# Preparing the scan operators of a two-layer hybrid backbone on VectorE alone, beside the Fourier mixer, with other amounts of gate work beside the scan of layer two

## The chip, the core and the metric

One core of a Trainium2 chip runs the kernel. The metric is the time of one execution in microseconds on the device, the median of several. Lower is better. The engines are TensorE (PE; its weight loads are listed as PEld), VectorE (DVE), ScalarE (ACT), GpSimd (POOL) and SyncE (SP), which here issues the DMA transfers.

## What is computed

Two layers work on 256 context tokens and 512 latent tokens of width 1024. Each layer normalises its tokens, projects them once, and feeds four mixers: A, latent attention; B, a Fourier transform over tokens and channels; C, a diagonal state space in both directions (S5); D, retention. Each mixer's 256 columns go through a branch matrix, are multiplied by a sigmoid gate, and are summed:

```python
o = jnp.stack([o_a, o_b, o_c, o_d], axis=2)
y = jnp.einsum('blnw,nwd->blnd', o, w_branch)
g = jax.nn.sigmoid(gates.reshape(B, L, N_BRANCH, D_MODEL))
return jnp.sum(g * y, axis=2) @ w_out
```

A residual and a squared-ReLU feed-forward part of width 4096 follow. Mixer C is the one that the change touches:

```python
lam = lax.complex(lam_re, lam_im);  step = jnp.exp(log_step)[:, None]
lam_bar = jnp.exp(lam * step)
b_bar = ((lam_bar - 1.0) / lam)[..., None] * lax.complex(b_re, b_im)
bu = jnp.einsum('blgh,gph->blgp', u, b_bar)        # 16 groups of 16 channels, 64 states
_, xs = lax.associative_scan(linear_recurrence_op, (lam_bar, bu), axis=1)
y = einsum(xs_f, c_f).real + einsum(xs_b, c_b).real + d * u
val, gate = jnp.split(gelu(y) @ w_glu, 2, axis=-1);  out = val * sigmoid(gate)
```

## The kernel before

**Matrix products.** A float32 product is made of three products of rounded parts. A weight tile `raw` comes by DMA from SyncE, ScalarE rounds it to `whi`, VectorE subtracts to `wlo` (`split`, line 300). Gates use tiles of 128x1024 (`raw`, `whi`, `wlo`); branch matrices use 128x256 (`raws`, `whis`, `wlos`), and there is one buffer of `raws`, so the next transfer waits until both parts of the last are made. In layer 0 a gate is 48 matmuls; in layer 1, where only the latent tokens are kept, 24. A branch tile (`br`) is 12 and 6.

**Merging a mixer.** `merge_steps` is a generator that makes, for one mixer, a gate (matmuls, then a tanh on ScalarE) or a branch tile (matmuls, then VectorE's `gate<-gate,mm` or `xy<-gate,mm`, and, except for the first mixer, GpSimd's `xy<-xy,gate`) at each step. The argument `lead` says how many gates are made before the first branch tile. TensorE fills gaps of other stages with such steps.

**The scan.** The state space is done in chunks of eight tokens with 96 chunks. For each of eight groups (two of the reference's groups each) it needs small operators: `R` (128x288), `Wr` and `Wi` (128x256, made from Vr, Vi, wr, wi), a strip `ks`, all written to DRAM, and the rotation factors `er`, `ei` (16 x 96 per partition) of all groups, made by doubling: 1, 2, 4, 8, 16, 32 and again 32 columns, each in six products and sums with `gr`, `gi`, which are then squared. `s5_scalars` makes the small parameters (`par`), `s5_rot` the rotations, `s5_ops` the operators. In `s5_ops`, `first(g)` is the VectorE and GpSimd part, `second(g)` the TensorE and ScalarE part: eight products into one PSUM tile, then four transposes into another, both from `pb`, a pool of two buffers named `b`.

**Which engine.** Lines 1503 to 1535 give 10 of 16 columns of each longer rotation step to VectorE and 6 to GpSimd; `first` gives `Wi` to GpSimd (`e2`), and `second` the two sums of `ks`.

**Where it stands in the order.** `self.bg` is a background generator and `tick(n)` takes n of its steps; a scheduler orders each engine's instructions from there. Layer 0: `s5_prep`, which takes one step of the rotation and one of the operators by turns, runs under `merge_b`, the merge of mixer B behind the Fourier mixer (about 97 to 200 us). Behind it come `ada`, the other modulation rows (line 497), on VectorE too. Layer 1: `prepare(1)` runs in the feed-forward part of layer 0; there `f2`, the second product, also takes its accumulators `b` from `pb`, and VectorE adds them as `xy<-b,mod,xy`. In the scan itself (`s5`), `S5_STEPS[l][i]` steps of merges A and C are taken beside each group i; `early` is how many gates of merge C may be made there, before the scan's output exists. What is left of merge C follows the scan.

Of the kernel before, what the change touches and what calls it, by code (L numbers as in the profile page):

```python
# [33 lines left out]
FH = 258  # L34
# [6 lines left out]
S5_STEPS = ((2, 2, 1, 2, 1, 2, 1, 2, 1, 1, 1, 1), (2, 2, 2, 2, 2, 2, 2, 2, 2, 1, 1, 1))  # L41
# [174 lines left out]
class Net:  # L216
# [283 lines left out]
    def start(self, sp, prm):  # L500
# [38 lines left out]
        def scalars():  # L539
            for _ in range(4):  # L540
                next(later)
# [117 lines left out]
    def layer(self, l):  # L659
# [8 lines left out]
        with tc.tile_pool(name=f"mix{l}", bufs=1) as mp:  # L668
# [28 lines left out]
            early = 7 if last else 3  # L697
# [127 lines left out]
    def prepare(self, l):  # L825
# [16 lines left out]
    def merge_steps(self, l, n, o, segs, lead=1):  # L842
# [7 lines left out]
        for m in range(KT + lead - 1):  # L850
            if m < KT:
# [3 lines left out]
                g = Cols(self.mp.tile([128, NTOK - self.c0], F32, name="gate", bufs=7 if last else 3), self.c0)  # L855
# [27 lines left out]
    def fnet(self, l, sp, segs, o, gates):  # L883
# [31 lines left out]
        next(gates)  # L915
        T = {}
# [18 lines left out]
        for t in range(2):  # L935
            self.ahead['fl', t] = self.chunk(('fl', t), [sp.tile([128, 2 * FH], F32R, name=f"f{x}{t}") for x in ("hi", "lo")])
        next(gates)
        for s0, s1 in segs:
# [18 lines left out]
            for j in range(2):  # L957
# [10 lines left out]
                self.split(o[j][0][:, s0:s1], o[j][1][:, s0:s1], v)  # L968
        next(gates)
# [370 lines left out]
    def s5_scalars(self, l, sp):  # L1340
# [34 lines left out]
        self.tt(qi, qi, t0, OP.mult)  # L1375
        qb = lambda t: t[:, :, None].to_broadcast([128, 16, 16])
# [30 lines left out]
    def s5_prep(self, l, sp):  # L1407

        nc = self.nc
        bc = sp.tile([128, 2, 16, 16], F32, name="bc")  # L1410
        nc.sync.dma_start(bc, self.s5p[l][:, 512:])
        par = sp.tile([128, 16 * NPAR + 48], F32, name="par")
        nc.sync.dma_start(par, self.par[l])
        pr, pi, wr, wi, Br, Bi, Vr, Vi, rot = self.par_views(par)
# [5 lines left out]
        todo = [self.s5_rot(l, sp, rot), self.s5_ops(l, sp, bc, pr, pi, wr, wi, Br, Bi, Vr, Vi, dd)]  # L1420
        while todo:
            for t in list(todo):
                if next(t, 0) is None:
                    yield
                else:
                    todo.remove(t)

    def s5_ops(self, l, sp, bc, pr, pi, wr, wi, Br, Bi, Vr, Vi, dd):
        nc = self.nc
# [3 lines left out]
        def first(g):  # L1433
            gs = slice(2 * g, 2 * g + 2)
            e1, e2 = nc.vector, nc.gpsimd
# [5 lines left out]
            self.tt(Rr, c4(0), s4(pr), OP.mult, e1)  # L1441
            self.tt(t[0], c4(1), s4(pi), OP.mult, e1)
            self.tt(Rr, Rr, t[0], OP.subtract, e1)
            self.tt(Ri, c4(0), s4(pi), OP.mult, e1)
            self.tt(t[1], c4(1), s4(pr), OP.mult, e1)
            self.stt(Ri, Ri, -1.0, t[1], OP.mult, OP.subtract)

# [12 lines left out]
        def second(g, R, Wr, Wi):  # L1460
# [269 lines left out]
```

## Time and profile before

| | us |
|---|---|
| median of 3 runs | 2232.37 |
| lowest and highest | 2227.95, 2234.98 |
| the profiled execution | 2233.41 |
| its span | 2231.6 |
| TensorE busy | 2150.9 |
| VectorE busy | 1443.6 |
| ScalarE busy | 760.8 |
| GpSimd busy | 242.2 (283 instructions) |

The span is that of the profile; the execution's own time is longer by 1.8 us. TensorE is at 2.4 GHz when its granted clock is written as 1.00 and at 1.2 GHz when it is 0.50; values between are means over a stretch. The mean over the span is 0.988.

### The profile page before, as it was taken

The page shows a single profiled execution, that of the slowest core. Times are in us where ns is not written, and L with a number is a line of the kernel's source. Part 1 is how long each engine was busy: PE and PEld are TensorE (multiplying, and loading weights), DVE is VectorE, ACT ScalarE, POOL GpSimd, SP SyncE. Part 2 cuts the span into 40 slices and gives each one's busy share as a digit, 9 for nine tenths or more (in the row PEclk, how much of TensorE's full clock was granted, in tenths as well). Part 3 has the DMA queues.
Part 4 walks back from the last instruction along what each step waited for, and adds up shares of the span by engine and source line. Part 5 has one row for each costly group of instructions (what it writes and reads, how often), then busy time and mean ns, then how long its engine had stood idle before and what let it go on. Part 6 is the DMA issues. An engine that isn't in the chain of part 4 may idle for free.

```text
span 2231.6 us, 32342 instructions
## 1 busy us (share of the span) xinstructions
PE 2150.9 (96%) x12366; PEld 1828.5 (82%) x12366; DVE 1443.6 (65%) x3215; ACT 760.8 (34%) x1306; POOL 242.2 (11%) x283
## 2 busy tenths in 40 slices
PE   7988999999999999999999999999999989999999
PEld 1877987888888888888878788987788869888887
DVE  6587889976735576676885447568746656544454
ACT  2322433444433332121222235434534434222322
POOL 2062001100212000000131101100011111000000
PEclk8999999999999999999999999999999999999999
DMA  8345233313323145545232332112134332333332
GB/s 268 110 121 147 81 109 118 124 48 116 95 80 119 66 142 161 168 128 177 97 110 77 93 119 81 43 54 78 53 120 120 112 114 74 98 101 96 95 95 94
DMA packets 117769, 239.93 MB, mean 108 GB/s; under 512 B 16208, under 2 KB 45552, under 8 KB 117616
## 3 DMA queue, kind: packets, MB, share of 16 engines
q1 hardware_dynamic: 117616, 237.89, 34.3%
q8 instruction: 97, 1.59, 0.3%
q14 instruction: 56, 0.46, 0.1%
HBM read 218.29 MB, written 19.55 MB: 107 GB/s over the span
## 4 chain that ended last, share of the span: by engine, by line
PE 76%; DVE 13%; issue 5%; DMA 3%; ACT 3%; POOL 1%; SPq 0%; ACTq 0%; POOLq 0%; DVEq 0%
PE mm L245 48%; PE b L245 25%; PE b L248 3%; DVE wlo L300 1%; DVE olo L497 1%; DVE xy L261 1%; DVE R L251 1%; ACT whi L299 1%; DMA raw<-wst 1%; DMA adp<-wst 0%; POOL hlo L251 0%; ACT tmp L264 0%; DVE gate L261 0%; DMA par<-par 0%; DVE er L251 0%
## 5 line engine op out<-in xcount | busy, mean ns | idle before, releaser
L245 PE MATMUL mm<-hhi,wlo 128*128 128x256 f32 (+1 forms) x1768 | 533.2, 356 | 6.1 <-DVE wlo L300 4.5
L245 PE MATMUL mm<-hlo,whi 128*128 128x256 f32 (+1 forms) x1768 | 532.9, 355 | 3.3 <-POOL hlo L251 3.2
L245 PE MATMUL mm<-hhi,whi 128*128 128x256 f32 (+1 forms) x1768 | 532.4, 355 | 0.0
L300 DVE TENSOR_TENSOR wlo<-raw,whi 128x1024 fp32r<-128x1024 f32 (+2 forms) x233 | 292.2, 1255 | 161.8 <-ACT whi L299 161.2
L245 PEld LDWEIGHTS mm<-hhi,wlo 128*128 128x128 f32 x1768 | 331.1, 189 | 54.2 <-issue 4.0
L245 PEld LDWEIGHTS mm<-hlo,whi 128*128 128x128 f32 x1768 | 332.6, 189 | 51.5 <-POOL hlo L251 6.2
L245 PEld LDWEIGHTS mm<-hhi,whi 128*128 128x128 f32 x1768 | 332.5, 189 | 46.2
L299 ACT ACTIVATE whi<-raw 128x1024 fp32r<-128x1024 f32 (+2 forms) x233 | 243.2, 1046 | 370.8 <-PE b L245 307.7
L245 PE MATMUL b<-uh,wlo 128*128 128x256 f32 (+1 forms) x704 | 215.3, 360 | 9.6 <-DVE xy L261 6.6
L261 DVE SCALAR_TENSOR_TENSOR xy<-b,mod,xy 128x256 f32<-128x256 f32 (+1 forms) x192 | 121.9, 659 | 149.0 <-PE b L245 148.9
L245 PE MATMUL b<-ul,whi 128*128 128x256 f32 (+1 forms) x704 | 215.6, 359 | 0.1
L245 PE MATMUL b<-uh,whi 128*128 128x256 f32 (+1 forms) x704 | 215.0, 359 | 0.0
L245 PEld LDWEIGHTS b<-uh,wlo 128*128 128x128 f32 x704 | 132.4, 190 | 34.0 <-DVE xy L261 6.9
L251 DVE TENSOR_TENSOR tmp<-tmp 128x768 f32<-128x768 f32 (+1 forms) x64 | 52.8, 824 | 163.9 <-ACT tmp L264 163.9
L245 PEld LDWEIGHTS b<-ul,whi 128*128 128x128 f32 x704 | 132.8, 189 | 21.1 <-DVE ul L300 0.8
L264 ACT ACTIVATE tmp<-mm 128x768 f32<-128x768 f32 (+3 forms) x86 | 51.5, 599 | 289.0 <-PE mm L245 269.8
L245 PEld LDWEIGHTS b<-uh,whi 128*128 128x128 f32 x704 | 133.0, 189 | 20.0
L251 POOL TENSOR_TENSOR xy<-xy,gate 128x768 f32<-128x768 f32 (+1 forms) x48 | 84.6, 1765 | 544.3 <-DVE gate L261 449.8
L245 PE MATMUL mm<-whi,hlo 128*128 128x256 f32 (+1 forms) x424 | 122.9, 290 | 0.6 <-ACT tmp L264 0.6
L245 PE MATMUL mm<-wlo,hhi 128*128 128x256 f32 (+1 forms) x424 | 122.1, 288 | 0.6 <-DVE wlo L300 0.5
L245 PE MATMUL mm<-whi,hhi 128*128 128x256 f32 (+1 forms) x424 | 121.8, 287 | 0.0
L264 ACT ACTIVATE gate<-mm 128x768 f32<-128x768 f32 (+1 forms) x64 | 45.0, 702 | 150.9 <-PE mm L245 142.7
(459 smaller groups left out, 3365.5 us busy)
## 6 DMA issues: line engine op xcount, KB each, us to landing
raw<-wst SPq DMA_DIRECT2D x236, 512.0 KB
adr<-wst SPq DMA_DIRECT2D x96, 256.0 KB
olo<-wst SPq DMA_DIRECT2D x42, 256.0 KB
adp<-wst SPq DMA_DIRECT2D x32, 256.0 KB
raws<-wst SPq DMA_DIRECT2D x64, 128.0 KB
xy<-xT SPq DMA_DIRECT2D x16, 384.0 KB
ohi<-wst SPq DMA_DIRECT2D x22, 256.0 KB
oB<-scr SPq DMA_DIRECT2D x16, 294.0 KB
```

The lines of the kernel that those rows point to most:

```text
L245: return self.nc.tensor.matmul(out, a, b, start=start, stop=stop)
L248: self.nc.tensor.transpose(out, a, self.ident[:n, :n])
L251: (eng or self.nc.vector).tensor_tensor(out=out, in0=a, in1=b, op=op)
L261: (eng or self.nc.vector).scalar_tensor_tensor(out, a, s, b, op0=op0, op1=op1)
L264: self.nc.scalar.activation(out, a, f, **kw)
L299: self.last_hi = self.nc.scalar.activation(hi, src, AF.Copy)
L300: return (eng or self.nc.vector).tensor_tensor(out=lo, in0=src, in1=hi.bitcast(F32), op=OP.subtract)
L497: self.nc.vector.tensor_tensor_reduce(out=junk, in0=r, in1=c[:, v], scale=1.0, scalar=0.0, op0=OP.mult, op1=OP.add, accum_out=acc[:, v:v + 1])
```

## The change

Nothing that is computed changes. In layer 0 the rotations run under the Fourier mixer (`fnet` has new `tick` calls) and the operators alone under `merge_b`; in layer 1 all rotations come before all operators. GpSimd has no part in either: rotation steps are 16 columns wide on VectorE, and `Wi` and the sums of `ks` are on VectorE. `first` is two steps, `s5_scalars` eight instead of four. `second` puts its transposes into the upper half of each bank of the PSUM tile that its products use. To make room, the Fourier mixer's second table reuses the buffers of its folded input (`u`). In layer 1, four gates of merge C instead of seven are made beside the scan, with four buffers, and three of its groups take one step instead of two.

```diff
-S5_STEPS = ((2, 2, 1, 2, 1, 2, 1, 2, 1, 1, 1, 1), (2, 2, 2, 2, 2, 2, 2, 2, 2, 1, 1, 1))
+S5_STEPS = ((2, 2, 1, 2, 1, 2, 1, 2, 1, 1, 1, 1), (2, 2, 2, 2, 1, 2, 1, 2, 1, 1, 1, 1))
...
-            with tc.tile_pool(name=f"fn{l}", bufs=1) as sp:
-                self.fnet(l, sp, segs, o_b, merge_b)
-            self.dump2(f'ob{l}', o_b)
-            self.bg = iter(())
+            with tc.tile_pool(name=f"rot{l}", bufs=1) as rp:
+                self.bg = iter(()) if l else self.s5_prep(l, rp)
+                with tc.tile_pool(name=f"fn{l}", bufs=1) as sp:
+                    self.fnet(l, sp, segs, o_b, merge_b)
+                self.dump2(f'ob{l}', o_b)
+                self.tick(99)
+                self.bg = iter(())
+                if l == 0:
+                    with tc.tile_pool(name="sp0", bufs=1) as sp:
+                        self.bg = self.s5_ops(l, sp)
+                        self.tick(2)
+
+                        for i, _ in enumerate(merge_b):
+                            self.tick(1 if i % 2 else 3)
+                        self.tick(99)
...
-            early = 7 if last else 3
+            early = 4 if last else 3
...
-            for i, _ in enumerate(self.s5_prep(l, sp)):
-                yield
-                if i % 2:
-                    yield
+            yield from self.s5_prep(l, sp)
+            yield from self.s5_ops(l, sp)
...
-                g = Cols(self.mp.tile([128, NTOK - self.c0], F32, name="gate", bufs=7 if last else 3), self.c0)
+                g = Cols(self.mp.tile([128, NTOK - self.c0], F32, name="gate", bufs=4 if last else 3), self.c0)
...
-            self.ahead['fl', t] = self.chunk(('fl', t), [sp.tile([128, 2 * FH], F32R, name=f"f{x}{t}") for x in ("hi", "lo")])
+            self.ahead['fl', t] = self.chunk(('fl', t), [sp.tile([128, NTOK if t else 2 * FH], F32R, name=f"u{k}" if t else f"fl{k}") for k in range(2)])
+        self.tick()
         next(gates)
+        self.tick(2)
...
-            self.tt(Wi, b4(Vi), w4(wr), OP.mult, e2)
-            self.tt(t[1], b4(Vr), w4(wi), OP.mult, e2)
-            self.tt(Wi, Wi, t[1], OP.add, e2)
-            return R, Wr, Wi
+            self.tt(Wi, b4(Vi), w4(wr), OP.mult)
+            self.tt(t[1], b4(Vr), w4(wi), OP.mult)
+            self.tt(Wi, Wi, t[1], OP.add)
+            made.append((R, Wr, Wi))
...
-            self.tt(k0, k0, dd[:, 2 * g:2 * g + 2], OP.add, nc.gpsimd)
-            self.tt(ks[:, :, 7], ks[:, :, 7], k0, OP.add, nc.gpsimd)
-
-            p = self.pb()
+            self.tt(k0, k0, dd[:, 2 * g:2 * g + 2], OP.add)
+            self.tt(ks[:, :, 7], ks[:, :, 7], k0, OP.add)
+
             for k, W in enumerate((Wr, Wi)):
                 for q in range(2):
-                    self.tr(p[:, 256 * k + 128 * q:256 * k + 128 * q + 128], W[:, q].rearrange("p s h -> p (s h)"))
+                    o = 512 * k + 256 + 128 * q
+                    self.tr(p[:, o:o + 128], W[:, q].rearrange("p s h -> p (s h)"))
...
-                for s, e in ((slice(0, 10), nc.vector), (slice(10, 16), nc.gpsimd)) if m > 2 else ((slice(0, 16), nc.vector),):
-                    bb = lambda t: t[:, s, 0:1].to_broadcast([128, s.stop - s.start, m])
...
+                bb = lambda t: t[:, :, 0:1].to_broadcast([128, 16, m])
```

**First place: VectorE under `merge_b` of layer 0.** In the kernel before, these rows stand between the result of a branch tile (`xy<-gate,mm`) and the next branch weights (`wlos`). Here is one rotation step of 16 columns on 10 of 16 groups (`er`, `ei`, `ce`) and the squaring of the factor (`gr`, `gi`, `cg`):

```order
L251 TENSOR_TENSOR er<-er,gr 128x10x16
L251 TENSOR_TENSOR ce_1223<-ei,gi 128x10x16
L251 TENSOR_TENSOR ei<-ei,gr 128x10x16
L251 TENSOR_TENSOR er<-er,ce_1223 128x10x16
L251 TENSOR_TENSOR ce_1224<-er,gi 128x10x16
L251 TENSOR_TENSOR gr<-gr 128x16
L251 TENSOR_TENSOR cg_1239<-gi 128x16
L251 TENSOR_TENSOR ei<-ei,ce_1224 128x10x16
L251 TENSOR_TENSOR gr<-gr,cg_1239 128x16
L251 TENSOR_TENSOR gi<-gi,gr 128x16
L251 TENSOR_TENSOR cg_1240<-gr,gi 128x16
L300 TENSOR_TENSOR wlos<-raws,whis 128x256
```

In the changed kernel the rotation steps stand further forward, in the Fourier mixer, between the splits of its intermediate (`tlo`) and of its second table (`u<-raw,u`):

```order
L251 TENSOR_TENSOR er<-er,gr 128x16x32
L251 TENSOR_TENSOR gi<-gi,cg_962 128x16
L251 TENSOR_TENSOR ei<-ei,gr 128x16x32
L300 TENSOR_TENSOR tlo_816<-b,thi_815 128x512
L251 TENSOR_TENSOR ce_991<-ei,gi 128x512
L251 TENSOR_TENSOR ce_992<-er,gi 128x512
L300 TENSOR_TENSOR tlo_828<-mm,thi_827 128x512
L300 TENSOR_TENSOR tlo_837<-b,thi_836 128x512
L300 TENSOR_TENSOR u_859<-raw,u_858 128x516
L251 TENSOR_TENSOR er<-er,ce_991 128x16x32
L251 TENSOR_TENSOR ei<-ei,ce_992 128x16x32
```

The rotation rows have gone from the stretch that feeds the branch tiles to the stretch ahead of it, and are 16 groups wide.

**Second place: VectorE in the feed-forward part of layer 0**, where layer 1's operators are made. Before, the accumulators of `f2` (`xy<-b,mod,xy`) stand behind a run of 48 rows, which ends so:

```order
L251 TENSOR_TENSOR R<-bc,par 128x288
L251 TENSOR_TENSOR gi<-gi,cg_10751 128x16
L251 TENSOR_TENSOR cr_10787<-bc,par 128x288
L251 TENSOR_TENSOR Wr<-par 128x256
L261 SCALAR_TENSOR_TENSOR R<-R,cr_10787 128x288
L251 TENSOR_TENSOR cw_10796<-par 128x256
L261 SCALAR_TENSOR_TENSOR xy_7300<-b,mod_73,xy_7300 128x256
L251 TENSOR_TENSOR Wr<-Wr,cw_10796 128x256
L261 SCALAR_TENSOR_TENSOR xy_7300<-b,mod_73,xy_7300 128x512
L261 SCALAR_TENSOR_TENSOR xy_7301<-b,mod_73,xy_7301 128x256
L261 SCALAR_TENSOR_TENSOR xy_7301<-b,mod_73,xy_7301 128x512
```

In the changed kernel the rotation comes first, alone, and the adds of `f2` stand between its steps; a run is some twenty-five rows, of which the last are shown:

```order
L251 TENSOR_TENSOR ce_10824<-ei,gi 128x16x2
L251 TENSOR_TENSOR ce_10825<-er,gi 128x16x2
L251 TENSOR_TENSOR gr<-gr 128x16
L251 TENSOR_TENSOR er<-er,ce_10824 128x16x2
L251 TENSOR_TENSOR ei<-ei,ce_10825 128x16x2
L251 TENSOR_TENSOR cg_10834<-gi 128x16
L261 SCALAR_TENSOR_TENSOR xy_7266<-b,mod_73,xy_7266 128x256
L261 SCALAR_TENSOR_TENSOR xy_7266<-b,mod_73,xy_7266 128x512
L251 TENSOR_TENSOR gr<-gr,cg_10834 128x16
L251 TENSOR_TENSOR gi<-gi,gr 128x16
L251 TENSOR_TENSOR cg_10835<-gr,gi 128x16
```

The operators (`R`, `Wr`) no longer stand between the rotation and the adds; they come later, beside `f1`.

**Third place: VectorE at the end of layer 1's last merge.** In the kernel before, all gates are made and branch tile follows branch tile (`wlos`, then `gate<-gate,mm`); `hlo` is the split of the merged sum for the next product. TensorE has 42 matmuls of branch tiles in a row there, seven tiles:

```order
L300 TENSOR_TENSOR wlo<-raw,whi 128x1024
L261 SCALAR_TENSOR_TENSOR gate<-gate,mm 128x512 x2
L261 SCALAR_TENSOR_TENSOR hlo_17484<-xy_13102,hhi_17483 128x512
L300 TENSOR_TENSOR wlos<-raws,whis 128x256
L261 SCALAR_TENSOR_TENSOR hlo_17486<-xy_13103,hhi_17485 128x512
L261 SCALAR_TENSOR_TENSOR hlo_17488<-xy_13104,hhi_17487 128x512
L261 SCALAR_TENSOR_TENSOR gate<-gate,mm 128x512
L300 TENSOR_TENSOR wlos<-raws,whis 128x256
L261 SCALAR_TENSOR_TENSOR hlo_17490<-xy_13105,hhi_17489 128x512
L261 SCALAR_TENSOR_TENSOR gate<-gate,mm 128x512
L300 TENSOR_TENSOR wlos<-raws,whis 128x256
```

In the changed kernel a gate's `wlo` stands behind each `wlos` for as long as gates are left; TensorE has 6 matmuls of a tile and 24 of a gate by turns, and 24 of four tiles at the end:

```order
L261 SCALAR_TENSOR_TENSOR gate<-gate,mm 128x512
L300 TENSOR_TENSOR wlos<-raws,whis 128x256
L261 SCALAR_TENSOR_TENSOR gate<-gate,mm 128x512
L300 TENSOR_TENSOR wlos<-raws,whis 128x256
L300 TENSOR_TENSOR wlo<-raw,whi 128x1024
L261 SCALAR_TENSOR_TENSOR gate<-gate,mm 128x512
L300 TENSOR_TENSOR wlos<-raws,whis 128x256
L300 TENSOR_TENSOR wlo<-raw,whi 128x1024
L261 SCALAR_TENSOR_TENSOR gate<-gate,mm 128x512
L300 TENSOR_TENSOR wlos<-raws,whis 128x256
L300 TENSOR_TENSOR wlo<-raw,whi 128x1024
```

Three gates have moved from beside the scan to between these tiles.

## Rows read from the trace of the kernel before

**Rows 1.** Part 1 of the page: busy time, share of the span, instructions.
```profile
PE 2150.9 (96%) x12366; PEld 1828.5 (82%) x12366; DVE 1443.6 (65%) x3215; ACT 760.8 (34%) x1306; POOL 242.2 (11%) x283
```

**Rows 2.** Timeline of TensorE, 124 to 202 us: start, duration, [idle before <-releaser].
```profile
129.74 0.55 PE L245 MATMUL mm<-ohi,wlos 128*128 128x256 f32 x1 [3.61 <-DVE wlos L300]
...
149.32 0.84 PE L245 MATMUL mm<-hhi,wlo 128*128 128x256 f32 x2 [2.35 <-DVE wlo L300]
...
181.32 0.98 PE L245 MATMUL mm<-ohi,wlos 128*128 128x256 f32 x2 [3.92 <-DVE wlos L300]
```

**Rows 3.** Stretches of layer 0: busy us (instructions), PEclk, DMA share, GB/s.
```profile
95.00:205.00 110.00, 98.14 (x635) 83.08 (x634) 87.37 (x217) 27.52 (x59) 49.47 (x70) 0.92 0.49 146
130.00:135.00 5.00, 5.00 (x24) 3.79 (x25) 5.00 (x15) 2.06 (x3) 5.00 (x1) 0.50 0.29 72
150.00:155.00 5.00, 5.00 (x23) 4.36 (x22) 3.25 (x6) 0.42 (x1) 0.00 (x0) 0.71 0.72 172
180.00:185.00 5.00, 3.67 (x12) 3.22 (x12) 3.72 (x9) 0.42 (x1) 0.00 (x0) 0.52 0.63 132
```

**Rows 4.** Timeline of VectorE, 124 to 153 us: start, duration in us.
```profile
133.55 0.48 DVE L251 TENSOR_TENSOR ce<-ei,gi 128x320 f32<-128x320 f32 x1
133.95 0.48 DVE L251 TENSOR_TENSOR ei<-ei,gr 128x320 f32<-128x320 f32 x1
...
140.28 3.10 DVE L251 TENSOR_TENSOR er<-er,ce 128x320 f32<-128x320 f32 x1
...
146.55 0.45 DVE L251 TENSOR_TENSOR cr<-bc,par 128x288 f32<-128x288 f32 x1
146.92 0.41 DVE L251 TENSOR_TENSOR Wr<-par 128x256 f32<-128x256 f32 x1
147.26 0.45 DVE L261 SCALAR_TENSOR_TENSOR R<-R,cr 128x288 f32<-128x288 f32 x1
```

**Rows 5.** Timeline of GpSimd, 120 to 153 us.
```profile
129.94 5.69 POOL L251 TENSOR_TENSOR ei<-ei,gr 128x192 f32<-128x192 f32 x1
...
140.42 0.50 POOL L251 TENSOR_TENSOR ce<-ei,gi 128x192 f32<-128x192 f32 x1
```

**Rows 6.** The stretch of the Fourier mixer, layer 0, same columns as rows 3.
```profile
75.00:95.00 20.00, 20.00 (x129) 17.96 (x129) 5.97 (x9) 6.38 (x11) 0.00 (x0) 1.00 0.34 116
```

**Rows 7.** Waits of TensorE, 1075 to 1155 us: total, times, longest.
```profile
PE b L245 <- DVE xy L261: 6.6, 1, 6.6
PE mm L245 <- DVE wlo L300: 0.9, 1, 0.9
```

**Rows 8.** Waits of TensorE, 1155 to 1300 us.
```profile
PE b L245 <- ACT ks L264: 2.0, 2, 1.8
PE b L248 <- DVE xy L261: 1.3, 5, 0.3
```

**Rows 9.** Stretches of the feed-forward part of layer 0.
```profile
1120.00:1125.00 5.00, 5.00 (x25) 4.35 (x24) 3.85 (x19) 0.00 (x0) 3.63 (x6) 0.77 0.00 0
1240.00:1245.00 5.00, 5.00 (x25) 4.33 (x25) 4.32 (x11) 0.00 (x0) 0.38 (x1) 0.83 0.54 160
```

**Rows 10.** Waits of TensorE, 1640 to 1860 us.
```profile
PE mm L245 <- DVE wlos L300: 8.5, 4, 4.5
PE b L245 <- DVE tmp L261: 2.7, 1, 2.7
```

**Rows 11.** Stretches of layer 1, scan branch and last merge.
```profile
1750.00:1755.00 5.00, 5.00 (x19) 4.27 (x20) 4.84 (x10) 2.12 (x5) 0.00 (x0) 0.66 0.35 105
1815.00:1820.00 5.00, 3.87 (x9) 2.59 (x10) 2.19 (x4) 0.76 (x2) 1.30 (x1) 0.52 0.54 171
1820.00:1825.00 5.00, 3.52 (x11) 2.00 (x9) 1.94 (x4) 1.68 (x3) 1.35 (x2) 0.80 0.34 100
```

**Rows 12.** Timeline of VectorE, 1805.5 to 1829 us.
```profile
1818.47 0.42 DVE L300 TENSOR_TENSOR wlos<-raws,whis 128x256 fp32r<-128x256 f32 x1
...
1822.51 0.42 DVE L300 TENSOR_TENSOR wlos<-raws,whis 128x256 fp32r<-128x256 f32 x1
```

More of the change, by code (lines that the diff above doesn't have):

```diff
@@ L539, in scalars @@
         def scalars():
-            for _ in range(4):
+            for _ in range(8):
                 next(later)
@@ L1350, in s5_scalars @@
         pr, pi = T("pr", [16, 9]), T("pi", [16, 9])
+        yield
         step, _ = self.expm1(sp, lst, "st")
+        yield
         ang, dec = T("ang", [2, 16]), T("decs", [2, 16])
@@ L1407, in s5_prep, with s5_ops @@
     def s5_prep(self, l, sp):
+        par = sp.tile([128, 16 * NPAR + 48], F32, name="par")
+        self.nc.sync.dma_start(par, self.par[l])
+        *v, rot = self.par_views(par)
+        self.views = v
+        yield from self.s5_rot(l, sp, rot)
+    def s5_ops(self, l, sp):
         nc = self.nc
+        pr, pi, wr, wi, Br, Bi, Vr, Vi = self.views
         bc = sp.tile([128, 2, 16, 16], F32, name="bc")
         nc.sync.dma_start(bc, self.s5p[l][:, 512:])
-        par = sp.tile([128, 16 * NPAR + 48], F32, name="par")
-        nc.sync.dma_start(par, self.par[l])
-        pr, pi, wr, wi, Br, Bi, Vr, Vi, rot = self.par_views(par)
         dd = sp.tile([16, 16, 16], F32, name="dd")
@@ L1419, in s5_prep @@
         self.tt(dd, dd, self.ident[:16, None, :16].to_broadcast([16, 16, 16]), OP.mult)
[L1420 to L1429, printed above, removed]
         F, B = slice(0, 64), slice(64, 128)
@@ L1440, in first @@
             t = [T(f"cr{k}", [2, 9, 16]) for k in range(2)]
[L1441 to L1445, printed above, removed]
+            self.tt(Rr, c4(0), s4(pr), OP.mult)
+            self.tt(t[0], c4(1), s4(pi), OP.mult)
+            self.tt(Rr, Rr, t[0], OP.subtract)
+            self.tt(Ri, c4(0), s4(pi), OP.mult)
+            self.tt(t[1], c4(1), s4(pr), OP.mult)
             self.stt(Ri, Ri, -1.0, t[1], OP.mult, OP.subtract)
+            yield
             Wr, Wi = T("Wr", [2, 8, 16], 3), T("Wi", [2, 8, 16], 3)
@@ L1493, in s5_ops @@
             if g < 8:
-                made.append(first(g))
+                yield from first(g)
                 yield
@@ L1517, in s5_rot @@
             for o in range(0, min(n, NCH - n), m):
-                t = [T(f"ce{k}", [16, 32], 1) for k in range(2)]
+                t0, t1 = (T(f"ce{k}", [16, 32])[:, :, :m] for k in range(2))
                 i, j = slice(o, o + m), slice(n + o, n + o + m)
-                for s, e in ((slice(0, 10), nc.vector), (slice(10, 16), nc.gpsimd)) if m > 2 else ((slice(0, 16), nc.vector),):
-                    bb = lambda t: t[:, s, 0:1].to_broadcast([128, s.stop - s.start, m])
-                    t0, t1 = t[0][:, s, :m], t[1][:, s, :m]
-                    self.tt(er[:, s, j], er[:, s, i], bb(gr), OP.mult, e)
-                    self.tt(t0, ei[:, s, i], bb(gi), OP.mult, e)
-                    self.tt(er[:, s, j], er[:, s, j], t0, OP.subtract, e)
-                    self.tt(ei[:, s, j], ei[:, s, i], bb(gr), OP.mult, e)
-                    self.tt(t1, er[:, s, i], bb(gi), OP.mult, e)
-                    self.tt(ei[:, s, j], ei[:, s, j], t1, OP.add, e)
+                bb = lambda t: t[:, :, 0:1].to_broadcast([128, 16, m])
+                self.tt(er[:, :, j], er[:, :, i], bb(gr), OP.mult)
+                self.tt(t0, ei[:, :, i], bb(gi), OP.mult)
+                self.tt(er[:, :, j], er[:, :, j], t0, OP.subtract)
+                self.tt(ei[:, :, j], ei[:, :, i], bb(gr), OP.mult)
+                self.tt(t1, er[:, :, i], bb(gi), OP.mult)
+                self.tt(ei[:, :, j], ei[:, :, j], t1, OP.add)
             if n < 64:
@@ L1533, in s5_rot @@
             n *= 2
-            if n > 4:
-                yield
-        for _ in range(4):
             yield
```

20 lines of the change are left out of this document (9 added, 11 removed).

## The prediction

> **What bounds the kernel now.** I read the busy times first [rows 1]: TensorE works for 2150.9 us of a span of 2231.6, so all that an edit of the preparation can give back is the 80.7 us in which it stands, and what its clock loses after standing. GpSimd works for 242.2 us, which alone would be no reason to touch it. Next I read which waits of TensorE end on work that the change moves, stretch by stretch. Three stretches hold four tenths of the idle time.
>
> The first is layer 0 from 95 to 205 us. TensorE works for 98.14 of 110 us [rows 3], so 11.86 are idle, and 3.61 + 2.35 + 3.92 = 9.9 of them end on a split of weights by VectorE, before 130, 149 and 181 us [rows 2]. A split is short; what makes it late is its place in VectorE's queue, behind rotation and operator rows. After a stand the clock is low: 0.50 at 130 to 135 us, 0.71 at 150 to 155 and 0.52 at 180 to 185 [rows 3]. In work done at a lower clock that is 5.00 x 0.50 + 5.00 x 0.29 + 3.67 x 0.48 = 5.7 us lost.
>
> The second is the feed-forward part of layer 0: 6.6 and 0.9 us at 1075 to 1155 [rows 7], 2.0 and 1.3 where the operators' PSUM tiles and those of `f2` follow each other [rows 8]; 10.8 together, and 5.00 x 0.23 + 5.00 x 0.17 = 2.0 for the clock [rows 9].
>
> The third is layer 1: 2.7 us in the scan branch, and 8.5 us where seven branch tiles follow each other [rows 10]; 11.2 together, and 5.00 x 0.34 + 3.87 x 0.48 + 3.52 x 0.20 = 4.3 for the clock [rows 11].
>
> Last I read VectorE's rows beside GpSimd's. A row of 128x320 starts 0.40 us after the one before it when nothing is in the way, one of 128x288 takes 0.37 and one of 128x256 0.34 by the same reading [rows 4]. But `er<-er,ce` at 140.28 took 3.10 us. Through that time GpSimd ran rows of its own, like the one of 0.50 at 140.42 [rows 5]. The reverse stands there too: `ei<-ei,gr` on GpSimd at 129.94 took 5.69 us while VectorE's queue was full. The two engines keep each other out when both work on two operands in SBUF. So GpSimd's 49.47 us in the first stretch [rows 3] are not free work beside VectorE's 87.37; much of the latter is waiting.
>
> **The change, part by part.**
>
> *What VectorE gets.* From these starts [rows 4] I take 0.10 us plus 0.00094 us a column. A whole rotation is then six rows each of 16, 32, 64, 128, 256 and twice 512 columns: 6 x (0.12 + 0.13 + 0.16 + 0.22 + 0.34 + 0.58 + 0.58) = 12.8, and 36 rows for the factors at 0.12 = 4.3: 17 us in all. Of this, GpSimd's share was only columns, 0.00094 x 6 x 6 x 92 = 3.1 us. `Wi` is 24 rows at 0.34 = 8.2 us a layer. So VectorE gets 11.3 us a layer that GpSimd had, 22.6 in both.
>
> *Layer 0.* The rotation's 17 us now lie in the Fourier mixer. From 75 to 95 us VectorE works for 5.97 of 20 us and TensorE for all of it [rows 6]: 14.0 us are free, and the excess of 3.0 could push the mixer's splits back. Below, the stages before 75 us take part of it and it costs nothing; above, all 3.0. I take 2.5, near the upper end, because the two widest steps stand among `tlo` rows. Under `merge_b` only operators are left: 12 rows a group, six at 0.37 and six at 0.34, 4.3 us, against a gate and a branch tile of TensorE for each. Behind the mixer stands a block of some 40 of these rows, 15 us, but the first two branch tiles' weights and the next gate's are split ahead of it. So the wait before 130 us and that before 149 us should go. The one that ends at 181 us had `ada` rows in front; eleven of them still stand in one block ahead of a `wlos`. I keep that wait, 3.9, and 3.67 x 0.48 = 1.8 for the clock behind it. Gain: 11.9 + 5.7 - 3.9 - 1.8 = 11.9. Ends: 5 if two waits stay with their clock, 16 if nearly none does.
>
> *Layer 1's operators.* The accumulators of `f2` waited 6.6 us behind 48 rows of rotation and operators, with GpSimd between; a run is now about half as long and no row in it waits for GpSimd. The wait goes. With one PSUM tile a group instead of two, `f2` has to give up a buffer once, not twice; but ScalarE's copy of `ks` and that of the transposes now hold one tile one after the other, so I keep half of the 3.3 us [rows 8]. Gain: 10.8 + 2.0 - 1.6 = 11.2, ends 5 and 13.
>
> *Layer 1's tail.* There is one `raws` buffer. Two `wlos` of successive tiles start 4.04 us apart [rows 12], so seven tiles in a row are fed by transfer, ScalarE and VectorE in turn. Four waits belong to seven tiles: three ran before the first. With gates between, the transfer and the splits lie beside 24 matmuls; with four tiles at the end, three run and one waits, between 1.3 us (the mean of the three shorter waits, (8.5 - 4.5) / 3) and 4.5. I take 3.0, and 1.0 for the clock. The three gates that move do the same work later. The scan beside them has less cover: I keep nothing for it in the likeliest case, since its own wait of 2.7 us stands on a VectorE row queued behind splits of such gates. Gain: 11.2 + 4.3 - 3.0 - 1.0 = 11.5, ends 3 and 15.
>
> *Costs nothing in my sum:* the eight steps of `s5_scalars` (the same rows), the table in the buffers of `u` (its split stands behind the products that read `u`, with a gate's matmuls to cover it; 0.9 us, the wait on one such split [rows 7], if that cover is gone), and the stores of `er` and `ei` that SyncE now issues ahead of `merge_b`'s weights. The DMA share is 0.34 there [rows 6], so they have room.
>
> Sum: 11.9 + 11.2 + 11.5 - 2.5 = 32.1 us. The profiled execution took 2233.41 (span 2231.6 and 1.8 around it), which is 1.0 above the median. I forecast 2200.
>
> **The rivals.**
>
> *Layer 0 gives nothing.* The block of operators behind the mixer, or the `ada` rows, make `wlos` late as before, and only the place of the wait changes. For it: the block is 15 us long, and waits of 3.9 us come from less. Against: the splits ahead of it. It decides when a branch tile's `wlos` starts later than the end of the gate before it. Then 2200 + 12 = 2212.
>
> *Layer 1's tail gives nothing.* Four tiles at the end wait as seven did, or the scan with three gates fewer beside it makes TensorE stand. For it: 4.04 us a tile stays, and the scan's rows already wait behind GpSimd's sums. Then 2200 + 11.5 = 2212 as well.
>
> *Slower: VectorE was full and gets 22.6 us more.* If VectorE's long rows are not waits for GpSimd, then moving work there lengthens the two stretches in which it is the bound. The Trainium skill, Perfetto Trace Analysis, section Optimizing Scalar/DVE Operations, says that with VectorE saturated it may make sense to hand work to other engines, even GpSimd, and this change does the opposite; the same passage warns that the two share a read port and that it might not help. By its first half the sum is this: 2232 + 22.6 from the moved rows, less 11.5 for the tail, which does not depend on it: 2243. It decides at a row of 128x320 that still takes well over 0.48 us with GpSimd idle. Undisturbed rows of that shape last 0.48 already in the kernel before [rows 4], so I give it little.
>
> *It does not do what it says.* The same waits move to other releasers (DMA of `raws`, ScalarE's copies) and the time stays: 2232.
>
> **How the numbers follow.** A measurement of this kernel can tell a change from none at about 0.3%, 6.7 us. Forecast 0.56, its own range 2189 to 2211, by ends that do not all fall together. Layer 0 nothing 0.16; tail nothing 0.15; no change 0.07; slower 0.06. The first three are faster: 0.87. The range runs from 2187 to 2222: the upper end takes in both rivals at 2212 and part of their joint case at 2224; what is left out is no change and slower, 0.13, and a little at the low end.
>
> **What would show it.** GpSimd's busy time falls by more than half in 95 to 205 us, and VectorE's rotation rows of 512 columns take about 0.66 us (a row lasts 0.08 longer than the step to the next start [rows 4]), with none near 3. TensorE's idle time in that stretch is 3 to 5 us, the wait of 6.6 us on `xy` is gone, and the four last branch tiles hold one wait, not four. I would be wrong if a wait on `tlo` or `fe` stands in the mixer, if the scan of layer 1 shows TensorE waiting on VectorE for more than 5 us, or if `ada` rows stand before each late `wlos`.

## The result, and the profile after

| | before | after |
|---|---|---|
| median, us | 2231.41 (4 runs) | 2201.24 (4 runs) |
| lowest and highest | 2227.95, 2234.98 | 2199.32, 2204.08 |
| the profile's span | 2231.6 | 2200.6 |

The ratio is 0.9866, with a 95% interval of 0.9853 to 0.988: 30 us less, where 32 were forecast. The sum of the parts came out; two of the parts did not, as will be seen.

Part 1 of the page, for [rows 1]:

```profile
PE 2140.6 (97%) x12366; PEld 1821.4 (83%) x12366; DVE 1443.3 (66%) x3295; ACT 762.2 (35%) x1306; POOL 145.9 (7%) x143
```

VectorE has 80 rows more than before and its busy time is the same, 1443.3 us against 1443.6. It got GpSimd's rows (242.2 to 145.9 us there) and paid for them with time in which it had only been kept waiting. TensorE does the same 12366 matmuls in 10.3 us less, at a mean granted clock of 0.995 instead of 0.988, and stands 60.0 us instead of 80.7.

Where the 31.0 us of span went can be read by rows that both kernels have. VectorE's first `fe` of the Fourier mixer starts at 93.31 before and 93.08 after; its first `ul` (the feed-forward part of layer 0) at 802.29 and 789.60; its first `kl` of that stage's end at 1289.43 and 1264.91; the first memset of layer 1's scan at 1638.65 and 1613.03; the first `kl` behind the last merge at 1832.60 and 1799.74; its last `xy` at 2227.82 and 2196.75. So 0.2 us came from the mixer, 12.5 from the rest of layer 0 up to its feed-forward part, 11.8 from that part, 1.1 from layer 1 before its scan, 7.2 from the scan and the last merge, of which 1.8 were given back behind it. Of the 12.5, the first 12.3 are won by the time the retention of layer 0 begins (its first `gst` is at 245.84 before and 233.27 after), that is, under the merge beside which the operators are made. The stretch behind the last merge, which no run here edits, lasts from 395.1 to 397.6 us in the fourteen profiles of this study, so the 1.8 are no more than it varies by.

Stretches after, for [rows 3], [rows 6] and [rows 11] (busy us of PE, PEld, DVE, ACT, POOL, then clock, DMA share and GB/s):

```profile
75.00:95.00 20.00, 20.00 (x131) 18.09 (x130) 19.37 (x67) 6.56 (x13) 0.00 (x0) 1.00 0.41 134
95.00:205.00 110.00, 104.63 (x735) 90.34 (x734) 84.36 (x242) 33.74 (x73) 6.30 (x12) 1.00 0.49 143
1720.00:1725.00 5.00, 3.16 (x18) 2.91 (x17) 5.00 (x9) 1.83 (x5) 1.89 (x2) 0.78 0.38 114
1790.00:1795.00 5.00, 1.35 (x5) 1.11 (x6) 4.80 (x6) 1.68 (x3) 2.94 (x2) 0.94 0.54 161
1795.00:1800.00 5.00, 5.00 (x18) 3.95 (x17) 1.64 (x3) 1.58 (x2) 1.28 (x1) 0.72 0.39 105
```

From 95 to 205 us TensorE now stands 5.4 us instead of 11.9, at a clock of 1.00 instead of 0.92, and VectorE beside the Fourier mixer is busy for 19.37 of 20 us while TensorE, at 20.00, loses nothing there. In layer 1 two stretches with a stand are left, 1720 to 1725 and 1790 to 1795, and the clock there and behind them is 0.78 and 0.72 where it had been 0.66, 0.52 and 0.80. The rotation's rows beside the mixer, in the timeline of VectorE (start, duration):

```profile
81.63 0.68 DVE L251 TENSOR_TENSOR er<-er,gr 128x512 f32<-128x512 f32 x1
...
82.32 0.68 DVE L251 TENSOR_TENSOR ei<-ei,gr 128x512 f32<-128x512 f32 x1
82.92 0.68 DVE L300 TENSOR_TENSOR tlo<-b,thi 128x512 fp32r<-128x512 f32 x1
83.52 0.68 DVE L251 TENSOR_TENSOR ce<-ei,gi 128x512 f32<-128x512 f32 x1
```

A row of 512 columns lasts 0.68 us and the next starts 0.60 later; 0.66 and 0.58 had been worked out. None is near the 3.10 us of [rows 4]. The split `tlo` stands between them and TensorE does not wait for it.

Waits of TensorE from 95 to 215 us (total, times, longest), for [rows 2]:

```profile
PE b L248 <- ACT ks L264: 3.4, 5, 1.3
PE mm L245 <- DVE wlo L300: 1.1, 1, 1.1
PE mm L245 <- DVE rpt L261: 0.9, 1, 0.9
```

No wait on `wlos` is left; the largest is on ScalarE's copy of `ks`. The same view from 1040 to 1320 us, for [rows 7, 8]:

```profile
PE b L248 <- ACT ks L264: 1.4, 2, 0.7
PE b L245 <- DVE xy L261: 1.3, 5, 0.3
```

The wait of 6.6 us on `xy` is gone. And from 1600 to 1870 us, for [rows 10]:

```profile
PE mm L245 <- DVE wlos L300: 4.5, 1, 4.5
PE b L245 <- DVE tmp L261: 1.8, 1, 1.8
PE mm L245 <- ACT gate L264: 1.0, 1, 1.0
```

One wait on `wlos` instead of four is left at the end, but it is as long as the longest before. The scan's wait on `tmp` is 1.8 us where it was 2.7, and that on a gate's tanh, at the scan's start, rose from 0.5 to 1.0.

### The profile page after: what moved, and what is told of

Read it like the earlier page. It is cut to its first block, busy times and chain, and to the rows that moved or that the text cites. A ratio compares the mean times of both kernels' runs of the same rounds, so it can differ in the third digit from the quotient of the medians.

```text
span 2200.6 us, 32252 instructions
## 1 busy us (share of the span) xinstructions
PE 2140.6 (97%) x12366; PEld 1821.4 (83%) x12366; DVE 1443.3 (66%) x3295; ACT 762.2 (35%) x1306; POOL 145.9 (7%) x143
## 4 chain that ended last, share of the span: by engine, by line
PE 75%; DVE 9%; ACT 3%; issue 3%; DMA 2%; POOL 1%; SPq 0%; ACTq 0%; POOLq 0%; DVEq 0%
PE mm L245 46%; PE b L245 27%; PE b L248 3%; DVE wlo L300 1%; DVE olo L497 1%; ACT whi L299 0%; POOL hlo L251 0%; DMA raw<-wst 0%; ACT tmp L264 0%; DVE gate L261 0%; DVE xy L261 0%; DVE ob L251 0%; DVE tmp L256 0%; DMA raws<-wst 0%; POOL DT L251 0%
```

## The experiments

Each is timed against the kernel before on the same chip; the changed kernel's ratio is 0.9866 (0.9853 to 0.988). "The changed kernel" means the one above.

**Theory and rivals.** Theory: GpSimd and VectorE keep each other out, so that GpSimd's share made VectorE's rows long, and the long rows made weights late. First rival: the new places and steps gave the gain, and GpSimd was harmless. Second rival: VectorE was simply full.

**GpSimd's old share put back into the changed kernel.**

```diff
-            self.tt(Wi, b4(Vi), w4(wr), OP.mult)
-            self.tt(t[1], b4(Vr), w4(wi), OP.mult)
-            self.tt(Wi, Wi, t[1], OP.add)
+            self.tt(Wi, b4(Vi), w4(wr), OP.mult, nc.gpsimd)
+            self.tt(t[1], b4(Vr), w4(wi), OP.mult, nc.gpsimd)
+            self.tt(Wi, Wi, t[1], OP.add, nc.gpsimd)
...
+                for s, e in ((slice(0, 10), self.nc.vector), (slice(10, 16), self.nc.gpsimd)) if m > 2 else ((slice(0, 16), self.nc.vector),):
```

The two sums of `ks` get `nc.gpsimd` as well.

> The changed kernel with GpSimd's old share put back (Wi, 6 of 16 columns of the longer rotation steps, the two sums of ks); places, steps and PSUM tile stay as changed. If the two engines keep each other out (theory), VectorE's rows get longer again beside GpSimd's: 8 to 15 us slower than the changed kernel's 2201, so 2209 to 2216, with VectorE rows over 1 us among the operators. If only the new places gave the gain (rival), GpSimd's rows lie beside VectorE's and the time is 2201 within 2.

Measured: 2213.58 us, ratio 0.993 (0.9912 to 0.9947): by the medians 12 us of the 30 are lost, as the theory said. The other 18 stay with GpSimd at work, so the new places, the steps and the tail have a gain of their own; of the first rival only its second half, that GpSimd was harmless, is refuted. Rows of VectorE in layer 0's merge, and one of GpSimd:

```profile
141.13 0.98 DVE L251 TENSOR_TENSOR R<-R,cr 128x288 f32<-128x288 f32 x1
...
157.00 0.99 DVE L261 SCALAR_TENSOR_TENSOR R<-R,cr 128x288 f32<-128x288 f32 x1
```

```profile
113.21 2.90 POOL L251 TENSOR_TENSOR cw<-par 128x256 f32<-128x256 f32 x1
```

`R<-R,cr` lasts 0.98 and 0.99 us where 0.45 is undisturbed [rows 4]; no such row reached the 3.10 us of before. GpSimd's `cw` at 113.21 took 2.90 us while VectorE's queue was full. TensorE's waits from 95 to 215 us:

```profile
PE b L248 <- ACT ks L264: 7.5, 5, 5.4
```

They rose from 3.4 to 7.5 us, on the copy of `ks`. The longest of them begins with a late weight. These are rows of VectorE, SyncE, ScalarE and TensorE, and in the second fence the same `wlos` in the changed kernel:

```profile
121.88 0.41 DVE L300 TENSOR_TENSOR wlos<-raws,whis 128x256 fp32r<-128x256 f32 x1
122.31 0.47 SPq L270 DMA_DIRECT2D raws<-wst  x1
125.23 0.42 ACT L299 ACTIVATE whis<-raws 128x256 fp32r<-128x256 f32 x1 [6.89 <-DMA raws<-wst]
125.63 0.59 ACT L264 ACTIVATE ks<-b 16x256 f32<-16x256 f32 x2
126.28 0.69 PE L248 MATMUL b<-ident,Wr 128*128 128x128 f32 x2 [5.38 <-ACT ks L264]
```

```profile
116.65 0.41 DVE L300 TENSOR_TENSOR wlos<-raws,whis 128x256 fp32r<-128x256 f32 x1
```

`wlos` comes 5.2 us later than in the changed kernel; ahead of it, from 106 to 111 us, VectorE's rows of 256 columns last 0.73 to 0.96 us beside GpSimd's, where they last 0.42 in the changed kernel. The next `raws` is issued at its end, since there is one buffer; ScalarE stands 6.89 us for that transfer, with the copy of `ks` behind it in its queue; and the transposes, which share the PSUM tile, wait for the copy. So the theory's late weights are there, under the name of `ks`. By the landmarks of the section on the result, 6.9 us of the loss lie under the merge of layer 0 and 3.0 in its feed-forward part.

**Only `Wi` on GpSimd**, the first six lines of that diff alone.

> The changed kernel with only Wi back on GpSimd. Of the 12 us that GpSimd's whole old share cost, Wi is 24 of its rows a layer, in the stretch where VectorE has operators. If rows keep each other out one by one, most of it, 6 to 10 us slower than the changed kernel (2207 to 2211); if the rotations beside the mixer and f2 carried the cost, 1 to 4 (2202 to 2205).

Measured: 2211.12 us, 0.9906 (0.9893 to 0.992): 10 us slower than the changed kernel. Of GpSimd's share it is `Wi`, not the rotations, that costs most. With `Wi` alone on GpSimd the first `gst` of layer 0's retention comes 5.9 us later than in the changed kernel (239.20 against 233.27), 1.4 short of the 7.3 of the whole share (240.54). In layer 0 the rotations stand beside the mixer, where little is awaited. In the feed-forward part, where layer 1's stand among the adds of `f2`, the whole share costs 3.0 us and `Wi` alone nothing (478.3 and 475.1 us against 475.3 from the first `ul` to the first `kl`).

**The kernel before, without GpSimd in the preparation.**

```diff
-            e1, e2 = nc.vector, nc.gpsimd
+            e1 = e2 = nc.vector
...
-                for s, e in ((slice(0, 10), nc.vector), (slice(10, 16), nc.gpsimd)) if m > 2 else ((slice(0, 16), nc.vector),):
+                for s, e in ((slice(0, 16), nc.vector),):
```

The sums of `ks` go to VectorE too.

> The kernel before with its preparation on VectorE alone; order, steps, PSUM tiles and gates as before. Theory (port): much of VectorE's time was waiting, so 8 to 18 us faster than before, 2213 to 2223, with TensorE's waits on wlos in layer 0 and on xy in the feed-forward part mostly gone. Rival (VectorE was full): the 22.6 us that VectorE gets in addition show on the path, 2240 or more. Rival (place): without the new places no change, 2231 within 4.

Measured: 2227.71 us, 0.9988 (0.9978 to 0.9997). That is 4 us, half of the least that the theory allowed; the miss told the most of all runs. VectorE's rows in layer 0 (timeline), and two waits of TensorE:

```profile
139.10 0.67 DVE L251 TENSOR_TENSOR ei<-ei,ce 128x512 f32<-128x512 f32 x1
...
142.88 0.41 DVE L251 TENSOR_TENSOR cw<-par 128x256 f32<-128x256 f32 x1
143.22 0.94 DVE L261 SCALAR_TENSOR_TENSOR xy<-gate,mm 128x768 f32<-128x768 f32 x1
144.09 0.41 DVE L251 TENSOR_TENSOR Wi<-Wi,cw 128x256 f32<-128x256 f32 x1
144.42 1.21 DVE L300 TENSOR_TENSOR wlo<-raw,whi 128x1024 fp32r<-128x1024 f32 x1
```

```profile
145.77 0.98 PE L245 MATMUL mm<-hhi,wlo 128*128 128x256 f32 x2 [5.20 <-DVE wlo L300]
...
1129.15 0.98 PE L245 MATMUL mm<-hhi,wlo 128*128 128x256 f32 x2 [5.33 <-DVE wlo L300]
```

No row is long any more: `ei<-ei,ce` of 512 columns takes 0.67 us, `cw` 0.41. But the rows stand without a gap from 118 us on, and the `wlo` that TensorE waits for starts at 144.42 behind all of them; TensorE stood 5.20 us for it, and 5.33 at 1129 us in the same way. VectorE's own busy time fell a little, to 1441.8 us over the span, though it got 22.6 us of rows: the second rival, at 2243, is out. What stays is an order in which the free time cannot be used. So the engine and the order act together: 4 us for the engine in the old order, 12 in the new.

**Which part of the order.** First, layer 0's rotations under the merge again, all of them ahead of the operators, and nothing else.

```diff
-                self.bg = iter(()) if l else self.s5_prep(l, rp)
+                self.bg = iter(())
...
-                        self.bg = self.s5_ops(l, sp)
+                        self.bg = chain(self.s5_prep(l, rp), self.s5_ops(l, sp))
```

> The changed kernel with layer 0's rotations not beside the Fourier mixer but ahead of the operators under its merge, still on VectorE alone. Theory (the place matters once VectorE is alone): the 17 us of rotation rows stand ahead of the weights' splits again, 4 to 9 us slower than the changed kernel, 2205 to 2210, with waits on wlos or wlo before 150 us. Rival (only GpSimd made the rows long, the place is free): 2201 within 2.

Measured: 2202.68 us, 0.9869 (0.9855 to 0.9884): no difference that can be told. One long wait shows, late in the merge, and none of such length before 150 us:

```profile
173.00 0.59 PE L245 MATMUL mm<-ohi,wlos 128*128 128x256 f32 x2 [3.45 <-DVE wlos L300]
```

The place beside the mixer, the first thing the change does, is worth 0 to 3 us here; the profile gives 1.7 under the merge. The theory's 4 to 9 were wrong.

Second, rotation and operators by turns, as before, under the merge and in layer 1's preparation, with everything else as changed.

```diff
+        todo = [self.s5_prep(l, rp), self.s5_ops(l, sp)]
+        while todo:
+            for t in list(todo):
+                if next(t, 0) is None:
+                    yield
+                else:
+                    todo.remove(t)
```

> The changed kernel (VectorE alone, small steps, one PSUM tile, four gates) with rotation and operators taken by turns as in the kernel before: under the merge of mixer B in layer 0, and in layer 1's preparation. GpSimd's rows alone gave 3.7 us in the old order, and the new order with the rotation under the merge cost only 1.4. If taking them by turns is what made VectorE late without GpSimd: 2208 to 2214, with waits on wlo of 3 to 5 us near 145 and 1129 us. If the size of the steps did it: 2201 to 2205.

Measured: 2205.2 us, 0.9884 (0.9869 to 0.9899), 4 us slower by the medians, though the intervals overlap. The waits on `wlo` near 145 and 1129 us are not there; there is one on `wlos`:

```profile
173.61 0.83 PE L245 MATMUL mm<-ohi,wlos 128*128 128x256 f32 x2 [3.64 <-DVE wlos L300]
```

Third, the large steps of before with the rotation first and in the new place.

```diff
-                yield from first(g)
+                first(g)
-            yield
+            if n > 4:
+                yield
```

In `first`, the inner `yield` goes, and layer 1's steps are spread as in the kernel before.

> The changed kernel with the large steps of before (a group's twelve rows in one step, the first three doublings of the rotation in one, layer 1's steps spread as before), rotation still first and in the new place. If the size of the steps did it: 2208 to 2214. If the turns did it: 2201 to 2205.

Measured: 2209.55 us, 0.9901 (0.9884 to 0.9917), 8 us slower, clear of the changed kernel's interval. A `wlo` is late behind the operators' rows, which stand in VectorE's queue without a gap from 101 to 129 us:

```profile
130.01 0.98 PE L245 MATMUL mm<-hhi,wlo 128*128 128x256 f32 x2 [6.52 <-DVE wlo L300]
```

Small steps are the larger part of the order (8 us), turns the smaller (4, of which the place has a share, and not clear of the noise by themselves). The two together do not reach what the old order cost without GpSimd: 2227.71, less the tail's 8.5 us below, is 2219, 18 above the changed kernel. The landmarks show where the rest lies. Under layer 0's merge, from the first `fe` to the first `gst`, turns cost 3.6 us, large steps 5.7 and the old order 10.4, so there the two nearly make up the whole. In the feed-forward part they cost 1.8 each, and the old order 8.0. What is missing there may be that the two act together, or the other amounts of steps at each `tick`; no run separates these.

**Two PSUM tiles a group.**

```diff
+            p = self.pb()
             for k, W in enumerate((Wr, Wi)):
                 for q in range(2):
-                    o = 512 * k + 256 + 128 * q
-                    self.tr(p[:, o:o + 128], W[:, q].rearrange("p s h -> p (s h)"))
+                    self.tr(p[:, 256 * k + 128 * q:256 * k + 128 * q + 128], W[:, q].rearrange("p s h -> p (s h)"))
...
```

ScalarE's copy of the transposes is fitted to the new tile.

> The changed kernel with the transposes of each operator group in a PSUM tile of their own, as before. Theory: 1 to 3 us slower than the changed kernel, since TensorE's waits on ks move to the adds of f2. Rival: the single tile makes the transposes wait for the copy of ks (3.4 us of such waits in layer 0 of the changed kernel), so two tiles are 1 to 3 us faster.

Measured: 2198.39 us, 0.9853 (0.9837 to 0.9868), 3 us under the changed kernel with intervals that overlap. Waits of TensorE from 95 to 215 us:

```profile
PE mm L245 <- DVE rpt L261: 1.3, 2, 0.8
PE mm L245 <- DVE wlo L300: 1.1, 1, 1.1
PE mm L245 <- DVE xy L261: 0.9, 1, 0.9
```

The 3.4 us on `ks` are gone and nothing of that size took their place. The single tile is not shown to be a gain; more likely it costs 1 to 3 us, as the rival had it.

**Seven gates beside layer 1's scan**, with the old table of steps and seven buffers.

```diff
-            early = 4 if last else 3
+            early = 7 if last else 3
```

> The changed kernel with seven gates beside layer 1's scan and the old table of steps. The scan branch and the last merge of the two profiles differ by some 5.6 us, so theory: 2207 (5 to 7 us slower than the changed kernel), with four waits on wlos at the end, as before. If that part's gain came from earlier stages: 2201 within 2. By the prediction's own term of 11.5 us: 2213.

Measured: 2209.7 us, 0.9903 (0.9889 to 0.9918). The tail is worth 8.5 us by the medians; its profile ends 7.8 later than the changed kernel's (2204.52 against 2196.75). That is more than the 5 to 7 expected and less than the 11.5 of the prediction.

```profile
PE mm L245 <- DVE wlos L300: 8.5, 4, 4.5
PE b L245 <- DVE tmp L261: 2.9, 1, 2.9
```

The four waits are back, 8.5 us in all, and that on `tmp` is 2.9 us, longer than with four gates.

**What the last wait is.** In the changed kernel, VectorE's rows before the last wait on `wlos`, and GpSimd's sums beside them:

```profile
1787.32 2.32 DVE L300 TENSOR_TENSOR wlo<-raw,whi 128x1024 fp32r<-128x1024 f32 x1
...
1790.76 1.44 DVE L261 SCALAR_TENSOR_TENSOR hlo<-xy,hhi 128x512 fp32r<-128x512 f32 x1
1792.12 1.48 DVE L300 TENSOR_TENSOR wlos<-raws,whis 128x256 fp32r<-128x256 f32 x1
```

```profile
1787.22 1.34 POOL L251 TENSOR_TENSOR xy<-xy,gate 128x512 f32<-128x512 f32 x1 [5.38 <-DVE gate L261]
1790.38 2.94 POOL L251 TENSOR_TENSOR xy<-xy,gate 128x512 f32<-128x512 f32 x2 [1.82 <-DVE gate L261]
```

`wlo` takes 2.32 us where 1.2 is usual, `wlos` 1.48 instead of 0.42. The same stretched rows stand in the kernel before, ahead of the longest of its four waits there:

```profile
1808.75 2.32 DVE L300 TENSOR_TENSOR wlo<-raw,whi 128x1024 fp32r<-128x1024 f32 x1
...
1813.48 1.48 DVE L300 TENSOR_TENSOR wlos<-raws,whis 128x256 fp32r<-128x256 f32 x1
```

So the sums were put on VectorE, eight rows of the last merge (`None` stands for VectorE).

```diff
-                self.tt(self.y[m][:, a:b], self.y[m][:, a:b], g[:, a:b], OP.add, self.nc.gpsimd)
+                self.tt(self.y[m][:, a:b], self.y[m][:, a:b], g[:, a:b], OP.add, None if last and n == 2 else self.nc.gpsimd)
```

> The changed kernel with the eight sums of layer 1's last merge on VectorE instead of GpSimd. Theory (the one wait of 4.5 us left at the end is VectorE kept out by these sums: wlo 2.33, hlo 1.44, wlos 1.48 us beside them): wlo falls to 1.2 us, wlos to 0.42, the wait to 1 to 2.5 us, the time by 2 to 4 us to 2197 to 2199. Rival (the wait is the one raws buffer and its transfer): the wait stays at 4 to 5 us and the time at 2201, or rises by the 5 us of sums that VectorE gets.

Measured: 2199.01 us, 0.9849 (0.9833 to 0.9865). The wait and the rows:

```profile
PE mm L245 <- DVE wlos L300: 2.2, 1, 2.2
```

```profile
1788.89 1.22 DVE L300 TENSOR_TENSOR wlo<-raw,whi 128x1024 fp32r<-128x1024 f32 x1
1790.03 0.69 DVE L251 TENSOR_TENSOR xy<-xy,gate 128x512 f32<-128x512 f32 x1
...
1791.23 0.42 DVE L300 TENSOR_TENSOR wlos<-raws,whis 128x256 fp32r<-128x256 f32 x1
```

`wlo` and `wlos` are at 1.22 and 0.42 again, the sum itself takes 0.69, and the wait is halved. The rows and the wait moved as the theory said; the time is 2 us less, but the intervals overlap, so by itself it is not told from none. Of the 2.2 us that stay, ScalarE's row shows the cause:

```profile
1790.54 0.42 ACT L299 ACTIVATE whis<-raws 128x256 fp32r<-128x256 f32 x1 [1.50 <-DMA raws<-wst]
```

ScalarE waited for the transfer of `raws` until 1790.54, and `wlos` started 0.27 us after `whis` was made. All but about 0.3 us of what stays is thus the transfer into the one `raws` buffer, which the rival had made the cause of the whole wait.

**Both together**: two PSUM tiles and the last sums on VectorE.

> The changed kernel with two PSUM tiles a group and the last merge's sums on VectorE: the two edits touch different stages, so the gains should add: 2194 to 2198 by the theory, 2198 to 2201 if the sums on VectorE give nothing.

Measured: 2194.42 us, 0.9825 (0.9812 to 0.9839). This is clear of the changed kernel's interval, 7 us faster.

**Three gates instead of four**, on that version.

```diff
-            early = 4 if last else 3
+            early = 3
```

Three buffers and one step fewer beside the fourth group go with it.

> Two PSUM tiles, the last sums on VectorE (the version of 2194), and three gates instead of four beside layer 1's scan. If the tail still pays for each gate moved there: the wait of 2.2 us on wlos at the end goes and the time is 2190 to 2193. If the scan now lacks cover: TensorE waits there grow by 2 to 5 us and the time is 2195 to 2199.

Measured: 2197.05 us, 0.9846 (0.9832 to 0.9861), no gain; the intervals overlap. The wait of 2.2 us at the end is gone and another has come in the scan, in the timeline of TensorE:

```profile
1728.03 0.78 PE L245 MATMUL b<-oC,sX 128*96 128x128 f32 x4 [2.87 <-ACT sX L264]
```

It is 2.87 us on ScalarE's `sX`, the scan's result, where that wait was 0.4 with four gates: the scan now lacks the cover. The wait on `tmp` fell from 1.8 us to 0.2 in exchange. Three and four gates cannot be told apart by their times, and seven cost 8.5 us more than four.

**All sums of the merges on VectorE**, 40 more rows, on the version of 2194.

> The version of 2194 (two PSUM tiles, last sums on VectorE) with the other 40 sums of the merges on VectorE as well. If these sums keep VectorE out of rows that TensorE waits for, as in the last merge: 2188 to 2192. If they lie where nothing on VectorE is awaited, taking them out of the way gives nothing and the 0.6 to 0.9 us each that VectorE gets stays hidden: 2194 within 2; if it does not stay hidden, 2196 to 2200.

Measured: 2191.01 us, 0.9818 (0.9802 to 0.9834). This lies in the range of the first case, but cannot be told from 2194, so the choice between the first two stays open; the third is out. Part 1 of its page:

```profile
PE 2139.6 (98%) x12366; PEld 1821.3 (83%) x12366; DVE 1441.6 (66%) x3343; ACT 763.0 (35%) x1306; POOL 61.0 (3%) x95
```

VectorE's busy time is 1441.6 us with 48 rows more than in the changed kernel, less than the 1443.3 of the changed kernel itself, and GpSimd's is 61.0. The 48 sums did not make VectorE busier.

## Why the prediction was right, and where it was not

The forecast of 2200 met 2201. Its steps, in its order:

*What bounds the kernel, and the port.* Right. Rows lasted nearly as worked out, VectorE took 22.6 us of rows at no more busy time (and the 32 small sums of `ks`, which the working left out), and putting GpSimd back cost 12 us. These rows of GpSimd lie beside VectorE's `er<-er,ce` of 3.10 us at 140.28 [rows 4], behind the one of [rows 5]:

```profile
140.89 0.50 POOL L251 TENSOR_TENSOR ce<-er,gi 128x192 f32<-128x192 f32 x1
141.36 0.55 POOL L251 TENSOR_TENSOR er<-er,ce 128x192 f32<-128x192 f32 x1
```

The Trainium skill, Perfetto Trace Analysis, section Optimizing Scalar/DVE Operations, says both that a saturated VectorE may hand work to GpSimd and that this might not help because of the shared port; here the second half holds. The Trainium skill, SBUF — State Buffer, section Who interferes with whom, says that a VectorE instruction with two SBUF inputs contends with a GpSimd instruction that reads SBUF. The runs agree that the two contend (0.98 against 0.45 us). The same page of the Trainium skill, section SBUF: two separate sides, says that whichever starts first has the shared ports for its whole instruction and the other blocks. The runs show that a row can be kept out for longer than one instruction of the other engine: 3.10 us on VectorE beside GpSimd's rows of 0.50 to 0.55, and 2.90 and 5.69 us on GpSimd.

*The reason in layer 0.* The size was near (12.5 plus 0.2 against 11.9 less 2.5), the mechanism half told. That a split is late by "its place in VectorE's queue, behind rotation and operator rows" was right. But the working let the waits before 130 and 149 us go because the rotation's 17 us "now lie in the Fourier mixer" and only operators are left, and this step failed: with the rotations back under the merge those waits did not return and the time rose by 0 to 3 us. The runs showed that the engine alone gives 4 us in the old order, and that the small steps, which the working did not price at all, carry 8. The cost of 2.5 us in the mixer did not come: VectorE filled 19.37 of 20 us and no wait on `tlo` arose. The wait that was kept, 3.9 us at 181 us, went as well; 3.4 us on `ks` came in its stead. TensorE's idle time in the stretch is 5.4 us, a little above the 3 to 5 named as a sign.

*The feed-forward part.* 11.8 us against 11.2. The wait on `xy` and the low clock behind it went (the mean granted clock is 1.00 from 1040 to 1265 us, where it was 0.98 from 1040 to 1290). The single PSUM tile, which the sum let halve the waits there, is not shown to have given anything: they went from 3.3 us to 2.7, and with two tiles the whole was not slower.

*Layer 1's tail.* This was the term that was mis-sized: 11.5 us forecast, 5.4 net between the two profiles (7.2 less 1.8), 8.5 by the run with seven gates. Two steps of it failed. The one wait among the four tiles at the end was put at 3.0 us, with the 4.04 us between two `wlos` read as transfer, ScalarE and VectorE in turn: it was 4.5, and about half of it is made by GpSimd's sums, whose effect was seen in layer 0 and overlooked here; the 2.2 that stay without them are nearly all the transfer. And "its own wait of 2.7 us" on `tmp` was taken as gone: it is 1.8 with four gates and goes only with three (0.2), and that on a gate's tanh rose by 0.5.

*The sum* was right because layer 0 gave 3.3 us more than forecast, layer 1 before its scan 1.1 that no term held, and the feed-forward part 0.6 more, against 6.1 less from the tail: 1.1 less in all, as measured between the spans. The mechanism held in its main line, GpSimd's rows making VectorE's long and weights late, but that errors of 3 and 6 us cancelled to 1 is luck.

*The rivals.* "Layer 0 gives nothing", "VectorE was full" and "It does not do what it says" fell. "The tail gives nothing" fell, though a part of that term did. The condition named in it, a scan that lacks cover, came true at three gates, not at four.

## What to carry to other kernels

Before work is given to GpSimd beside VectorE, look at rows of one shape on either engine with and without the other at work: where they stretch, GpSimd's time is not free time, and here the rows went back at no cost in VectorE's busy time. But taking the contention away paid fully only where the freed time reached the row that someone waits for. So try background work in smaller steps: they were worth 8 us here, with six rows instead of twelve in most of them. And a wait carries the name of what ended last: that on `ks` began with a late `wlos`, three engines earlier. Work that fills one gap can leave another, and one run each way from the chosen amount shows whether there is more to gain.

## What the runs showed that was not expected

GpSimd can be starved as badly as VectorE: to the `ei<-ei,gr` of 5.69 us for 192 columns [rows 5] comes `cw`, 2.90 for 256 with the share put back, both while VectorE's queue was full. And VectorE's busy time stayed between 1439.7 and 1446.5 us in all fourteen profiles of this study, whichever rows GpSimd had: in these profiles, the time in which it is kept out counts as busy.
